# Feed-forward products of a two-layer trunk: columns walked in 14 orders, low parts of the weights at six starts

## The chip, the core and the metric

The kernel runs on one core of a Trainium2 chip. The metric is the device time of one execution in microseconds (us). The kernel before was timed twice: 1116.48 and 1116.37 us, median 1116.42 us. The core's engines are TensorE (PE: matmuls, and PEld: the loads of the stationary operand), VectorE (DVE), ScalarE (ACT), GpSimd (POOL) and SyncE (SP, which issues transfers).

## The reference

Two layers over a sequence of 512 tokens of width 1024, all in float32. Each layer has an attention part (stick-breaking heads and differential heads, one shared input and one shared output projection) and a feed-forward part. The change lies in the feed-forward part alone:

```python
h = rmsnorm(x, mlp_norm[l])
u = jnp.square(jax.nn.relu(jnp.einsum('bsd,df->bsf', h, w_ff1[l])))   # 1024 -> 4096
x = x + jnp.einsum('bsf,fd->bsd', u, w_ff2[l])                        # 4096 -> 1024
```

A final rmsnorm follows the second layer.

## The kernel before, in words

**Split operands.** Every float32 operand of a product is split into a high part, rounded to the type in which TensorE works here (`fp32r`), and a low part, the rest of it: `whi` and `wlo` for weights, `h_hi`/`h_lo` or `hxh`/`hxl` for the normed input and `Ah`/`Al` for the hidden values. A product is then three matmuls, high by high, high by low and low by high, accumulated in one PSUM tile. They are issued by the helper `three` (L298 to L304); so the three lines L302, L303 and L304 carry nearly all matmuls of the program, and the profile's groups are told apart by the tiles' names.

**Units.** The weights come in units of 128 x 1024 values. `_unit_list` (L53) writes their order out by hand, and the class `_Weights` (L95) loads, splits and hands them out in that order. `split_part` (L120) takes a pair of tiles from a pool, lets ACT write the high part (L118) and DVE the low part (L135). A low tile is 1152 columns wide, 128 more than a unit, so that the 1024 columns can begin at some column other than 0. Before, they begin at column 16 for the kinds `s` and `v` and at column 0 for all others (`NARROW`, `ASIDE`, L40, used in L128).

**The feed-forward part** works in four groups `g`, each of a quarter of the 4096 hidden values. Both products are made with seven multiplications of blocks in place of eight; the seven are the *forms* 11, x3, x2, 21, x1, x4 and 22.

- Group 0's first product is plain: units of kind `1`, 128x512 matmuls into tiles called `f`. The change doesn't touch them.
- First product of groups 1 to 3: units of kind `s`, 84 in all (two layers, three groups, two halves `j`, seven forms), in `quad_group` (L1050). Here the weights are stationary (128x128) and the normed input is moving: 256 columns, one row of a tile, without a gap. A unit makes 24 matmuls: two halves `pr` of the PSUM tile, four blocks of depth, three matmuls each. Sums go to the PSUM tiles X, V and Y.
- Second product, all groups: units of kind `f`, 112 in all (two layers, four groups, seven forms, two halves `c`), in the loop over `FORMS2` (L1235 on). Here the hidden values are stationary and the weights are moving: 512 columns. A unit makes 12 matmuls: two rows of weights, two blocks of tokens that go to two PSUM banks in turn, three matmuls each. Sums go to X, V, Y, W and, for the last unit pair, Z; the last pair's second block of tokens is cut into two halves of 256 columns (`part`).

**Order.** The program order of each engine is that of the code, with some edges added by hand (`behind`). After each unit's use `next` (L158) asks for the split of the unit that lies some units ahead; the loads of later weights hang on that split (`then`). In the attention part a planner with costs fills TensorE's queue; the feed-forward part has a fixed order.

**Matmuls in the attention part that the prediction uses as yardsticks.** L552 (`scores`) reads a moving operand of two runs of 128 columns that lie apart in SBUF, and writes 256 PSUM columns in one run. L302, L303, L683 and L684 with 128x512 into the tiles called `O0d` and `O0s` (`s3`) read two runs of 256 columns that lie 640 apart (`firsts`). L554 and L555 read one run. L441 and L442 (`values_of`) have the weights, units of kind `v`, as moving operand: L441 reads `wlo`, which begins at column 16, and L440 and L442 read `whi`, which begins at column 0.

Of the kernel before, what the change touches and what calls it, by code (L numbers as in the profile page):

```python
# [24 lines left out]
GROUPS = 4  # L25
# [11 lines left out]
MAN = ()  # L37
APART = (("s", 0, 1), ("s", 3, 0), ("s", 3, 1))
_CTX = {}
NARROW, ASIDE = "sv", 16  # L40
DLY_R, DLY_D, DLY_S, DLY_Q = 3.5, 10.2, 9.0, 6.0
TAIL, ATT, DENSE, CAP = 6.0, 53.0, 145.0, 0.1
FORMS = ("11", "x3", "x2", "21", "x1", "x4", "22")
FORMS2 = ("11", "x3", "21", "x2", "x1", "x4", "22")
# [40 lines left out]
_UNITS = _unit_list()  # L85


_INDEX = {u: i for i, u in enumerate(_UNITS)}
_RING = [i for i, u in enumerate(_UNITS) if u[0] not in "fs"]
_SLOT = {u: n for n, u in enumerate(_RING)}  # L90
# [4 lines left out]
class _Weights:  # L95
# [24 lines left out]
    def split_part(self, i, a, b):  # L120
        nc = self.nc
        if i not in self.tiles and i in self.home:
            self.tiles[i] = self.home[i]
        if i not in self.tiles:
            k = self.spot(i)
            self.owner[k] = i
            self.turn = k + 1
            at = ASIDE if _UNITS[i][0] in NARROW else 0  # L128
            hi = self.pools[k // 2].tile([P, 1024], F32R, tag="whi", name=f"whi{i}")
            lo = self.pools[k // 2].tile([P, 1152], F32R, tag="wlo", name=f"wlo{i}")[:, at : at + 1024]  # L130
            self.tiles[i] = (hi, lo)
        hi, lo = self.tiles[i]
        raw = self.first if (i, b) == (0, P) else self.raw[i]
        h = self.round(hi[:, a:b], raw[:, a:b])
        self.last = h, nc.vector.tensor_tensor(  # L135
            out=lo[:, a:b], in0=raw[:, a:b], in1=hi[:, a:b].bitcast(F32), op=ALU.subtract)
# [21 lines left out]
    def next(self, kind, alone=False):  # L158
        i = self.used
        assert _UNITS[i][0] in kind  # L160
        self.used += 1
        if i > 0 and not alone:
            self.do_split(i + 2 * len(self.pools), i)
        return self.tiles.pop(i)
# [3 lines left out]
def trunk(ctx, tc, opened, xT, w, w2, w1, gfin, lamv, cos, sin, out):  # L168
# [71 lines left out]
    def split(hi, lo, src):  # L240
        a = nc.scalar.activation(hi, src, AF.Copy)  # L241
        nc.vector.tensor_tensor(out=lo, in0=src, in1=hi.bitcast(F32), op=ALU.subtract)  # L242
        return a
# [51 lines left out]
            nc.tensor.transpose(pt[:, j * P : (j + 1) * P], col[:, j : j + 1].to_broadcast([P, P]), ident)  # L295
        nc.scalar.copy(bc, pt)

    def three(pt, a, b, first, last, goes_on=False):  # L298
        ah, al = a
        bh, bl = b  # L300
        return (
            nc.tensor.matmul(pt, ah, bh, start=first, stop=False, skip_group_check=goes_on),  # L302
            nc.tensor.matmul(pt, ah, bl, start=False, stop=False, skip_group_check=goes_on),  # L303
            nc.tensor.matmul(pt, al, bh, start=False, stop=last, skip_group_check=goes_on))  # L304
# [4 lines left out]
    def wpair(u, c, n=P):  # L309
        return u[0][:, c * n : (c + 1) * n], u[1][:, c * n : (c + 1) * n]  # L310
# [27 lines left out]
    for l in range(L):  # L338
        with ExitStack() as actx:
# [49 lines left out]
            first = W.split  # L389
# [459 lines left out]
            at = attn()  # L849
# [3 lines left out]
            for cost in dense(pts if l else None):  # L853
# [5 lines left out]
                while live and credit > 0:  # L859
                    c = next(at, None)  # L860
# [17 lines left out]
        with ExitStack() as fctx:  # L878
# [3 lines left out]
            last = l == L - 1  # L882
# [157 lines left out]
            def temp(k, name):  # L1040
                if k == 3:
                    return bank("o", name)
                while ring[0] % 3 != k:
                    bank("s", "skip")
                return bank("s", name)

            def chunk(j, k):
                return x[:, ((4, 5, 6, 7), (4, 5, 0, 1))[j][k], :]

            def quad_group(g, j, banks_):  # L1050
                nm = f"{l}{g}{j}"
                X, V, Y = (temp(k, f"{n}{nm}") for k, n in zip(banks_, "XVY"))
                sx, v3 = x[:, 2, :], x[:, 3, :]
                F = [chunk(j, k) for k in range(4)]
                both = x[:, 4:8, :].rearrange("p (a b) t -> p a b t", b=2)[:, :, 0, :]
                if j:
                    both = x.rearrange("p (a b) t -> p a b t", b=4)[:, :, 0, :]
                hi, lo = ([e[:, k, :, :].rearrange("p a t -> p (a t)") for k in range(7)] for e in sides[j])
                for form in FORMS:
                    u = W.next("s")  # L1060
                    to = {"x3": V, "x4": V, "21": Y}.get(form, X)
                    h = h_forms[form]
                    for pr in range(2):
                        for c in range(4):
                            at = 512 * pr + P * c
                            three(to[:, 256 * pr : 256 * pr + 256], (u[0][:, at : at + P], u[1][:, at : at + P]),
                                  (h[0][:, c, :], h[1][:, c, :]),
                                  form in ("11", "x3") and pr == c == 0, pr == 1 and c == 3, True)
                    if form == "11":
                        nc.scalar.copy(Y, X)  # L1070
                    elif form == "x3":
                        nc.scalar.copy(v3, V)
                    elif form == "x2":
                        nc.scalar.copy(sx, X)
                    elif form == "21":
                        nc.scalar.activation(F[1], Y, AF.Relu)
                        nc.scalar.activation(F[1], F[1], AF.Square)
                        split(hi[0], lo[0], F[1])
                    elif form == "x1":
                        nc.vector.scalar_tensor_tensor(  # L1080
                            out=F[2], in0=X, scalar=-1.0, in1=v3, op0=ALU.mult, op1=ALU.subtract)
                    elif form == "x4":
                        tt2(F[0], V, sx, ALU.add)
                        nc.scalar.activation(both, both, AF.Relu)
                        nc.scalar.activation(both, both, AF.Square)
                        split(hi[1], lo[1], F[2])
                        tt2(F[1], F[1], F[0], ALU.subtract)
                        tt2(F[0], F[2], F[0], ALU.subtract)
                        tt2(F[2], F[2], F[1], ALU.add)
                        split(sides[j][0][:, 3:5, :, :].rearrange("p k a t -> p (k a t)"),  # L1090
                              sides[j][1][:, 3:5, :, :].rearrange("p k a t -> p (k a t)"),
                              x[:, 4:6, :].rearrange("p c t -> p (c t)"))
                    else:
                        nc.scalar.activation(F[3], X, AF.Relu, scale=-1.0)
                        nc.scalar.activation(F[3], F[3], AF.Square)
                    if j and form in ("11", "x3", "x2"):
                        rest_of_forms(0, {"11": "21", "x3": "x2", "x2": "22"}[form])
# [112 lines left out]
            for g in range(GROUPS):  # L1210
# [24 lines left out]
                for form in FORMS2:  # L1235
                    total, to = SUMS[form], chains[CHAIN[form]]
                    opens = form == "11" or g == 0 and form in ("x3", "21")
                    if form == "x4" and not end:
                        to = [temp(k, f"W{l}{g}{k}") for k in (r_, s_)]
                        opens = True  # L1240
                    work = [(c, i, r, 0) for c in range(GP // 2) for i in range(2) for r in range(2)]
                    tail = end and form == "22"
                    if tail and last:
                        turned = gather(total, to)
                        to = [temp(k, f"Z{l}{k}") for k in (r_, s_)]
                        opens = True
# [9 lines left out]
                    for n, (c, i, r, part) in enumerate(work):  # L1256
                        if c not in held:
                            held[c] = W.next("f")
                        u = held[c]
                        hi, lo = (e[:, :, i, :] for e in sides[c])  # L1260
                        rs = slice(r * P, r * P + P)
                        mine = [m for m, e in enumerate(work) if e[2:] == (r, part)]
                        pt, b_ = to[r], wpair(u, i, 512)
                        if part:
                            pt = halves[part - 1][:, 0:256]
                            b_ = [e[:, 256 * part - 256 : 256 * part] for e in b_]
                        three(pt, (hi[:, SIDE[form], rs], lo[:, SIDE[form], rs]), b_,
                              opens and n == mine[0] and part < 2, n == mine[-1], not opens)
                        if tail and last and n == 3:
                            squares += [square(0, 0), seed, square(1, 0)]  # L1270
                            first += [weighed[2], turned[1], came[1], root(0), weighed[3], root(1), store(0, 0, False)]
                            squares.append(store(0, 1, True))
                            first += [*gather(total, to, (0,)), store(1, 0, False)]
                            squares += [square(2, 1), store(1, 1, True)]
                        if end and not last and form == "22" and n % 2:
                            h = back(n // 2)
                            rests.append(h[1])
                            halfway = h
# [21 lines left out]
                    elif end and last and form == "x4":  # L1300
                        first = [came[0]]
# [97 lines left out]
```

## Time and profile before

| what | value |
|---|---|
| median of the timed runs | 1116.42 us (1116.37 to 1116.48) |
| the profiled execution's own time | 1116.32 us |
| its span, first to last instruction | 1114.6 us |
| TensorE matmuls | 6345, busy 1106.9 us |
| layer 1's feed-forward part on TensorE | 236.85 to 553.88 us |
| layer 2's feed-forward part on TensorE | 788.48 us to the end |

In the profile a group of instructions is given as line, engine, operation, written tile, read tiles, shape and count, then busy time in us and mean duration of one in ns, then the engine's idle time ahead of them. TensorE's matmuls overlap: one starts before the end that the profile models for its predecessor, so the *step* from one start to the next is what a matmul costs, and the duration is the step and a fixed tail.

### The profile page before, as it was taken

Reading aid. Unit: us, or ns where it says so; the run is one execution under the profiler, and the core shown is the slowest. Engines: PE = TensorE matmul, PEld = TensorE weight load, DVE = VectorE, ACT = ScalarE, POOL = GpSimd, SP = SyncE. Lnnn points to the kernel's source line nnn. Section 1 sums busy time; section 2 is a strip of 40 time slices with the busy share of each in tenths; the row PEclk is TensorE's granted clock in tenths of the full one; section 3 lists DMA queues with packets and bytes.
Section 4 is the critical chain, followed back from the end, with each engine's and each line's share of the span. In section 5 each row is a group of like instructions: output and inputs, shape, how many; then the busy total and the mean of one; then the engine's idle time right before and its main releaser. Section 6 shows DMA issues by size and latency. Waiting matters only on the chain.

```text
span 1114.6 us, 17170 instructions
## 1 busy us (share of the span) xinstructions
PE 1106.9 (99%) x6345; PEld 968.2 (87%) x6345; DVE 908.6 (82%) x1333; ACT 689.6 (62%) x1131; POOL 151.8 (14%) x233
## 2 busy tenths in 40 slices
PE   9999999999999999999999999999999999999997
PEld 6889889888899899899878898988888998998986
DVE  7799788898668779779877897897797787797797
ACT  6447767567558458467345576775774484674765
POOL 1001343101011001001000014430010010010010
PEclk9999999999999999999999999999999999999999
DMA  7476343269687778648325654512577886697462
GB/s 241 147 189 189 114 131 107 84 220 228 176 216 179 179 202 188 190 133 214 109 76 150 188 159 129 168 60 76 210 172 186 207 183 182 185 189 206 116 132 95
DMA packets 61044, 181.25 MB, mean 163 GB/s; under 512 B 7456, under 2 KB 8736, under 8 KB 60960
## 3 DMA queue, kind: packets, MB, share of 16 engines
q1 hardware_dynamic: 50160, 141.84, 40.2%
q0 software_dynamic: 10368, 37.75, 19.6%
q8 instruction: 50, 0.82, 0.3%
q10 hardware_dynamic: 432, 0.56, 0.1%
q14 instruction: 34, 0.28, 0.1%
HBM read 150.77 MB, written 4.19 MB: 139 GB/s over the span
## 4 chain that ended last, share of the span: by engine, by line
PE 96%; DVE 2%; issue 1%; DMA 0%; ACT 0%; POOL 0%; SPq 0%; POOLq 0%; DVEq 0%; ACTq 0%
PE X L302 9%; PE X L304 9%; PE X L303 9%; PE V L302 4%; PE V L304 4%; PE V L303 4%; PE wo L302 3%; PE wo L303 3%; PE wo L304 3%; PE f L304 3%; PE f L302 3%; PE f L303 3%; PE Y L304 2%; PE Y L303 2%; PE Y L302 2%; PE W L304 1%
## 5 line engine op out<-in xcount | busy, mean ns | idle before, releaser
L118 ACT ACTIVATE whi<-q 128x1024 fp32r<-128x1024 f32 x96 | 101.7, 1059 | 106.1 <-PE X L304 38.0
L135 DVE TENSOR_TENSOR wlo<-q,whi 128x1024 fp32r<-128x1024 f32 x96 | 117.2, 1222 | 44.6 <-ACT whi L118 44.3
L118 ACT ACTIVATE whi<-raw 128x1024 fp32r<-128x1024 f32 (+1 forms) x82 | 81.0, 994 | 34.5 <-issue 17.9
L135 DVE TENSOR_TENSOR wlo<-raw,whi 128x1024 fp32r<-128x1024 f32 (+1 forms) x82 | 96.7, 1186 | 6.7 <-ACT whi L118 6.4
L302 PE MATMUL X<-whi,Ah 128*128 128x512 f32 x248 | 97.5, 393 | 0.0
L303 PE MATMUL X<-wlo,Ah 128*128 128x512 f32 x248 | 96.6, 390 | 0.0
L304 PE MATMUL X<-whi,Al 128*128 128x512 f32 x248 | 96.6, 390 | 0.0
L135 DVE TENSOR_TENSOR wlo<-waves,whi 128x1024 fp32r<-128x1024 f32 x40 | 48.9, 1222 | 15.9 <-ACT whi L118 15.8
L118 ACT ACTIVATE whi<-waves 128x1024 fp32r<-128x1024 f32 x40 | 42.3, 1056 | 29.1 <-PE X L304 20.5
L302 PEld LDWEIGHTS X<-whi,Ah 128*128 128x128 f32 x248 | 46.5, 188 | 12.0 <-DVE y L1123 1.9
L304 PEld LDWEIGHTS X<-whi,Al 128*128 128x128 f32 x248 | 46.6, 188 | 9.9
L303 PEld LDWEIGHTS X<-wlo,Ah 128*128 128x128 f32 x248 | 46.6, 188 | 8.9
L304 PE MATMUL X<-h_hi,wlo 128*128 128x256 f32 x192 | 54.1, 282 | 0.0
L304 PE MATMUL X<-hxh,wlo 128*128 128x256 f32 x192 | 54.1, 282 | 0.0
L303 PE MATMUL X<-h_lo,whi 128*128 128x256 f32 x192 | 54.0, 281 | 0.0
L302 PE MATMUL X<-hxh,whi 128*128 128x256 f32 x192 | 54.0, 281 | 0.0
L303 PE MATMUL X<-hxl,whi 128*128 128x256 f32 x192 | 54.0, 281 | 0.0
L302 PE MATMUL X<-h_hi,whi 128*128 128x256 f32 x192 | 53.9, 281 | 0.0
L302 PE MATMUL f<-h_hi,whi 128*128 128x512 f32 x128 | 50.4, 393 | 0.0
L304 PE MATMUL f<-h_hi,wlo 128*128 128x512 f32 x128 | 49.9, 390 | 0.0
L303 PE MATMUL f<-h_lo,whi 128*128 128x512 f32 x128 | 49.8, 389 | 0.0
L242 DVE TENSOR_TENSOR Al<-x,Ah 128x512 fp32r<-128x512 f32 (+1 forms) x60 | 46.5, 792 | 3.7 <-ACT Ah L241 3.5
(764 smaller groups left out, 3693.3 us busy)
## 6 DMA issues: line engine op xcount, KB each, us to landing
raw<-in_w SPq DMA_DIRECT2D x78, 512.0 KB, 3.6
q<-in_w SPq DMA_DIRECT2D x48, 512.0 KB, 4.3
q<-in_w POOLq DMA_DIRECT2D x48, 512.0 KB, 7.8
waves<-in_w SPq DMA_DIRECT2D x28, 512.0 KB, 4.5
first_a<-in_w SPq DMA_DIRECT2D x12, 512.0 KB, 5.1
first_b<-in_w SPq DMA_DIRECT2D x12, 512.0 KB, 5.3
first_c<-in_w SPq DMA_DIRECT2D x12, 512.0 KB, 4.1
first_b<-in_w POOLq DMA_DIRECT2D x12, 512.0 KB, 6.3
```

The costliest lines, as they stand in the source:

```text
L118: return self.nc.scalar.activation(o, src, AF.Copy)
L135: self.last = h, nc.vector.tensor_tensor(out=lo[:, a:b], in0=raw[:, a:b], in1=hi[:, a:b].bitcast(F32), op=ALU.subtract)
L242: nc.vector.tensor_tensor(out=lo, in0=src, in1=hi.bitcast(F32), op=ALU.subtract)
L302: nc.tensor.matmul(pt, ah, bh, start=first, stop=False, skip_group_check=goes_on),
L303: nc.tensor.matmul(pt, ah, bl, start=False, stop=False, skip_group_check=goes_on),
L304: nc.tensor.matmul(pt, al, bh, start=False, stop=last, skip_group_check=goes_on))
```

## The change

Two things change, both for the units of kinds `s` and `f` alone.

1. **Orders of walking.** `three` gets an argument `way`. With it the columns of the PSUM tile and of the moving operand (high and low) are visited in another order, the same for both, so each product still lands in its own column. A way is (a, c, back): the columns are cut into runs of c neighbouring columns, and the runs are taken in order (a = 1), or interleaved from `a` stretches; `back` turns the order of the runs ("b"), of the stretches ("a"), or of the columns inside each run ("c", the only ways in which neighbouring columns are visited downwards). The number of matmuls, of columns and of bytes is as before. `WAYS1` serves the `s` units (256 columns), `WAYS2` the `f` units (512 columns); entry 0 of each is the old order.
2. **Starts of the low parts.** The low part of an `s` unit begins at column 0, 8, 16, 24, 32 or 64 of its tile, that of an `f` unit at 0, 8, 16 or 32. Kind `v` stays at 16, all others at 0.

`_turn_of` numbers the 84 `s` units as 14 ways times 6 starts, and the `f` units as 14 ways times 4 starts (the two halves `c` share one). The halves of the last unit pair (`part`) keep the old order.

```diff
-NARROW, ASIDE = "sv", 16
+ASIDE = 16
+WAYS1 = ((1, 256, ""), (1, 32, "b"), (2, 32, ""), (4, 32, ""), (2, 16, ""),
+         (2, 64, ""), (4, 8, ""), (2, 8, ""), (4, 16, ""), (1, 32, "c"),
+         (1, 64, "c"), (2, 32, "a"), (8, 16, ""), (2, 32, "b"))
+PLACES1 = (0, 8, 16, 24, 32, 64)
+WAYS2 = ((1, 512, ""), (1, 128, "b"), (2, 32, ""), (4, 32, ""), (2, 16, ""),
+         (2, 128, ""), (8, 32, ""), (2, 8, ""), (4, 64, ""), (1, 32, "c"),
+         (1, 128, "c"), (2, 64, "a"), (16, 16, ""), (1, 64, "b"))
+PLACES2 = (0, 8, 16, 32)
...
+def _turn_of(u):
+    l, g = u[1], u[2]
+    if u[0] == "s":
+        n = ((l * 3 + g - 1) * 2 + u[3]) * 7 + FORMS.index(u[4])
+        return WAYS1[n % len(WAYS1)], PLACES1[n // len(WAYS1)]
+    n = (l * GROUPS + g) * 7 + FORMS2.index(u[3])
+    return WAYS2[n % len(WAYS2)], PLACES2[n // len(WAYS2)]
...
-            at = ASIDE if _UNITS[i][0] in NARROW else 0
+            kind = _UNITS[i][0]
+            at = _turn_of(_UNITS[i])[1] if kind in "fs" else ASIDE if kind == "v" else 0
...
-    def three(pt, a, b, first, last, goes_on=False):
+    def walked(t, way):
+        a, c, back = way
+        if c == t.shape[-1]:
+            return t
+        if a == 1:
+            t = t.rearrange("p (b c) -> p b c", c=c)
+            return t[:, ::-1, :] if back == "b" else t[:, :, ::-1] if back == "c" else t
+        t = t.rearrange("p (a b c) -> p b a c", a=a, c=c)
+        return t[:, ::-1, :, :] if back == "b" else t[:, :, ::-1, :] if back == "a" else t
+
+    def three(pt, a, b, first, last, goes_on=False, way=None):
         ah, al = a
         bh, bl = b
+        if way:
+            pt, bh, bl = (walked(e, way) for e in (pt, bh, bl))
...
                             three(to[:, 256 * pr : 256 * pr + 256], (u[0][:, at : at + P], u[1][:, at : at + P]),
                                   (h[0][:, c, :], h[1][:, c, :]),
-                                  form in ("11", "x3") and pr == c == 0, pr == 1 and c == 3, True)
+                                  form in ("11", "x3") and pr == c == 0, pr == 1 and c == 3, True,
+                                  _turn_of(("s", l, g, j, form))[0])
...
-                              opens and n == mine[0] and part < 2, n == mine[-1], not opens)
+                              opens and n == mine[0] and part < 2, n == mine[-1], not opens,
+                              None if part else _turn_of(("f", l, g, form, c))[0])
```

## The prediction

> **What bounds the kernel now.** I read the page first: the busy times, the granted clock and the chain of work that ended last.
>
> ```profile
> span 1114.6 us, 17170 instructions
> ...
> PE 1106.9 (99%) x6345; PEld 968.2 (87%) x6345; DVE 908.6 (82%) x1333; ACT 689.6 (62%) x1131; POOL 151.8 (14%) x233
> ...
> PEclk9999999999999999999999999999999999999999
> ...
> PE 96%; DVE 2%; issue 1%; DMA 0%; ACT 0%; POOL 0%; SPq 0%; POOLq 0%; DVEq 0%; ACTq 0%
> ```
>
> TensorE is busy for 1106.9 of 1114.6 us, its clock is never held down (every slice of PEclk reads 9), and 96% of the chain runs through it. Busy does not mean at its peak, so next I cut the span at the seams of the feed-forward stages and read the busy time of each stretch. The columns are the stretch, its length, and then busy time and count for each engine; the last three are granted clock, DMA share and GB/s.
>
> ```profile
> 280.85:319.11 38.26, 38.26 (x169) 31.40 (x168) 24.96 (x26) 21.95 (x27) 3.50 (x4) 1.00 0.76 193
> 319.11:358.69 39.58, 39.58 (x338) 39.57 (x336) 30.02 (x32) 29.47 (x39) 5.32 (x7) 1.00 0.75 189
> ...
> 874.43:914.01 39.58, 39.58 (x338) 39.58 (x336) 31.29 (x34) 28.69 (x37) 5.29 (x7) 1.00 0.76 189
> 914.01:952.37 38.36, 38.36 (x170) 31.42 (x169) 31.58 (x35) 19.02 (x22) 3.41 (x4) 1.00 0.76 191
> ```
>
> The stretches from 280.85 and 914.01 are second products (`f` units, 14 units of 12 matmuls = 168); those from 319.11 and 874.43 are first products (`s` units, 14 of 24 = 336; the count of PE holds one or two neighbours that reach over the seam, that of PEld doesn't). In all four TensorE is busy for the whole length: no matmul waits for anything. So a nanosecond that a walked matmul gains or loses stands in the end time one for one, and whatever the other engines do inside their spare time is worth nothing.
>
> The prices follow. A 256-column matmul of an `s` unit costs 39.58 / 336 = 117.8 ns from start to start. A 512-column matmul of an `f` unit costs 38.26 / 168 = 227.7 ns. The difference, 109.9 ns for 256 columns, is 0.429 ns for a column; what is left of the short one, 117.8 - 109.9 = 7.9 ns, is fixed for each matmul. These are the two things on which a walk can act: time per column and time per instruction.
>
> **The change part by part.** It adds and removes no instruction, no transfer and no wait, and it moves none past another in any queue. It changes the address sequence of some matmuls and the address of some tiles.
>
> *How many.* Entry 0 of each list is the old order. Of 84 `s` units 6 keep it, so 78 x 24 = 1872 matmuls are walked. Of 112 `f` units 8 keep it; the other 104 make 1248, less 12 whose tokens are cut into unwalked halves: 1236. Together 3108 of 6345.
>
> *How many jumps.* A jump is a place where the next run doesn't follow the last one. A way with runs of c columns has 256/c - 1 or 512/c - 1 of them. Over the 14 ways that sums to 155 for `s` and 215 for `f`. Each way has 6 `s` units (144 matmuls) and 8 `f` units (96): 155 x 144 + 215 x 96 - 84 (the unwalked halves) = 42,876 jumps.
>
> *What a jump of the moving operand costs.* The trace has matmuls that already read two runs: L552 (two of 128, by the code) and the 128x512 ones into O0s and O0d (two of 256). Beside them stand one-run matmuls of the same sizes: L554 and L555 from the same stage, and the groups that the change touches.
>
> ```profile
> L552 PE MATMUL S0s<-st0s3k,st0s3q 128*128 128x256 f32 x2 | 0.6, 278 | 0.0
> L554 PE MATMUL S0s<-st0s3k,st0s3q 128*128 128x256 f32 x2 | 0.6, 281 | 0.0
> L683 PE MATMUL O0s<-turned,vs 128*128 128x512 f32 x5 | 2.0, 392 | 0.0
> L302 PE MATMUL O0d<-turned,vdh 128*128 128x512 f32 x4 | 1.6, 391 | 0.0
> L303 PE MATMUL O0d<-turned,vdh 128*128 128x512 f32 x4 | 1.6, 392 | 0.0
> L554 PE MATMUL S0s<-st0s3k,st0s3q 128*128 128x512 f32 x2 | 0.8, 393 | 0.0
> L555 PE MATMUL S0s<-st0s3k,st0s3q 128*128 128x512 f32 x2 | 0.8, 389 | 0.0
> ...
> L302 PE MATMUL X<-whi,Ah 128*128 128x512 f32 x248 | 97.5, 393 | 0.0
> L303 PE MATMUL X<-wlo,Ah 128*128 128x512 f32 x248 | 96.6, 390 | 0.0
> L302 PE MATMUL X<-hxh,whi 128*128 128x256 f32 x192 | 54.0, 281 | 0.0
> ```
>
> With one jump: 278 ns at 256 columns, 391 to 392 at 512. With none: 281, and 389 to 393. So a jump costs between -3 and +3 ns by single rows, and nothing that stands out of their scatter. I take 0: the mean is below it at 256 columns and within it at 512. A gain from jumps I exclude, since every column still has to pass. For the upper end I take 1 ns, about what the 512-column rows leave (391.7 on the mean of the three with a jump, 391 of L554 and L555): 42,876 x 1 ns = +42.9 us.
>
> *What the walked PSUM side costs.* No matmul of the trace writes its PSUM columns in more than one run, and none goes downwards, so no row prices this. The floor is 0, from the moving side just read: the array takes a column every 0.429 ns, and the write needs only to keep that pace. The ceiling by the nearest rows is a second pass of the columns, 109.9 ns for a 256-column matmul and 219.8 for a 512-column one; I keep it for the rivals. I take 0, because each run holds at least 8 neighbouring columns and the two-run rows show address generation keeping pace on the reading side. That is the weakest step of this prediction.
>
> *Two orders on one bank.* Consecutive units add into the same tile in different orders, so a column could be asked for again sooner than before. It is not: the three matmuls of one product share an order, an `s` unit ends in the second half of its tile while the next begins in the first, and an `f` unit alternates between two banks. Cost 0.
>
> *The starts.* An `s` unit's low part is stationary in L304. These are the weight loads of that line and of L302, and the moving low part in the `v` units:
>
> ```profile
> L304 PEld LDWEIGHTS X<-hxh,wlo 128*128 128x128 f32 x192 | 36.9, 192 | 0.0
> L302 PEld LDWEIGHTS X<-hxh,whi 128*128 128x128 f32 x192 | 36.0, 188 | 0.0
> L304 PEld LDWEIGHTS f<-h_hi,wlo 128*128 128x128 f32 x128 | 24.0, 188 | 5.1
> ...
> L441 PE MATMUL p0u<-wlo,h_hi 128*128 128x256 f32 x64 | 17.9, 280 | 0.0
> L442 PE MATMUL p0u<-whi,h_lo 128*128 128x256 f32 x64 | 17.9, 280 | 0.0
> ```
>
> Low parts that begin at column 16 load in 192 ns, those at 0 (`f<-h_hi,wlo`) in 188. If the start is the reason, and if the whole of it lies on the path, 70 of 84 units leave column 16: 70 x 8 x 4 ns = 2.2 us gained. If every other start loads like 16, nothing. I take 0 and keep -2.2 us as the lower bound, because one row cannot tell the start from the place in the triple. As a moving operand a low part at column 16 costs what a high part at 0 does (280 and 280 ns), so the `f` units' starts are free. For the writer:
>
> ```profile
> L135 DVE TENSOR_TENSOR wlo<-q,whi 128x1024 fp32r<-128x1024 f32 x96 | 117.2, 1222 | 44.6 <-ACT whi L118 44.3
> L135 DVE TENSOR_TENSOR wlo<-first_a,whi 128x1024 fp32r<-128x1024 f32 x24 | 29.4, 1225 | 20.6 <-ACT whi L118 20.6
> ```
>
> DVE writes at column 16 (`first_a`) in 1225 ns and at 0 (`q`) in 1222: 3 ns on some 200 writes, 0.6 us, covered by VectorE's spare 9.6 us in each stretch of 39.58 (30.02 busy). Without that cover it would be those 0.6 us.
>
> **Sum.** 0 (jumps) + 0 (PSUM) + 0 (order) + 0 (starts), on the profiled execution's own 1116.32 us: span 1114.6 and 1.7 around it. The median of the timed runs lies 0.1 above, so the forecast is 1116.4 us. Its own range is 1114 (2.2 for the starts) to 1121 (a quarter of a column, 0.107 ns, for each jump: 4.6 us). About 2%, 22.3 us here, is what a measurement of this kernel can tell from no change.
>
> **Rivals.**
>
> *Every jump costs a little.* One mechanism, the address generator restarting at each run, on reading or writing. At one column (0.429 ns) it is 18.4 us, 1134.8; at 1 ns 42.9 us, 1159.3. It decides from 22.3 us / 42,876 = 0.52 ns on. For it: the two-run 512 rows are a shade above some one-run rows. Against: L552 at 278 ns is below.
>
> *Downward columns pass at half pace.* Two of the 14 ways ("c") visit neighbouring columns downwards: 12 `s` units (288 matmuls) and 16 `f` units (192). If the PSUM write or the read takes neighbours in pairs and pairs only upwards, each pays a second pass: 288 x 109.9 ns + 192 x 219.8 ns = 73.9 us, 1190.2. It decides from 30% of such a pass on. For it: the trace has no downward matmul. Against: nothing but that no engine here shows a price for order as such. The Trainium skill, Advanced Engine Details and Errata, section PSUM Cachelines, wants "every two consecutive elements" to be contiguous; twelve ways satisfy that, and it doesn't say whether a downward pair does.
>
> *Every broken write passes at half pace.* All 3108 walked matmuls pay the second pass: 1872 x 109.9 ns + 1236 x 219.8 ns = 477.4 us, 1593.8. The same section also says that any non-contiguous access pattern slows matmuls significantly; by that sentence alone this rival holds, and no run here shows a broken PSUM write. Against: runs of 8 and more give the write the same neighbours as before, except once per run.
>
> *Faster.* If walking hid the fixed 7.9 ns of each walked matmul (say, by meeting a memory line that is free sooner), it would give 3108 x 7.9 = 24.6 us, 1091.8. Against: the two-run rows keep it; L552's 3 ns would be a third of it at best.
>
> *The change does nothing at all* gives the forecast's time too; it is part of the first case.
>
> **How the numbers follow.** Forecast 0.70; a price for each jump 0.12, a third of it below 0.52 ns and so within 2%; downward half pace 0.11; half pace for all 0.04; faster 0.03. Faster by over 2%: 0.03. Within: 0.70 + 0.04 = 0.74. Slower: 0.08 + 0.11 + 0.04 = 0.23. The range goes from 1113.5, the lower bound of the starts with half a microsecond for the repeat, to 1160, the price of 1 ns for each jump: 0.70 + 0.12 = 0.82 lie in it.
>
> **What would show it.** In the changed profile the same stages should have the same lengths (39.58 and 38.3 us), TensorE without idle time, and each group of L302, L303 and L304 the durations quoted. A price for each jump shows as units whose matmuls last longer the shorter their runs are, most in those with runs of 8. Downward half pace shows as two units in 14 at twice the step, and none elsewhere. A start that matters shows in the loads of L304 alone, 188 or 192 ns by unit. The forecast is wrong if the stretches grow, and which of the rivals is right is read from which units grow.

## The result, and the profile after

The changed kernel takes 1128.84 us (1128.74 to 1128.94), against 1116.42 before: a ratio of 1.0112, 95% interval 1.0095 to 1.0128. That is 12.4 us slower. It lies inside the range given, but the forecast was no change, and the kernel moved by more than its runs scatter. That it lies in the range is luck: the upper end came from a price for each jump, which the experiments below rule out as the cause.

The profile page of the changed kernel, the lines that answer to those of before:

```profile
span 1127.0 us, 17170 instructions
...
PE 1119.5 (99%) x6345; PEld 972.3 (86%) x6345; DVE 909.0 (81%) x1333; ACT 690.5 (61%) x1131; POOL 152.0 (13%) x233
...
PEclk9999999999999999999999999999999999999999
...
PE 99%; issue 0%; DVE 0%; POOL 0%; ACT 0%; POOLq 0%; DVEq 0%; ACTq 0%
```

The count of instructions is the same, the clock is the same, and TensorE's busy time has grown by 12.6 us, the span by 12.4. DVE and ACT have hardly grown (0.4 and 0.9 us, off the path). The stages, with the same columns as in the prediction:

```profile
280.75:319.94 39.19, 39.19 (x169) 31.50 (x168) 24.96 (x26) 22.00 (x27) 3.50 (x4) 1.00 0.74 191
319.94:360.14 40.20, 40.20 (x338) 40.19 (x336) 30.02 (x32) 29.57 (x39) 5.38 (x7) 1.00 0.75 187
...
881.48:921.56 40.08, 40.08 (x337) 40.08 (x336) 31.17 (x34) 28.85 (x37) 5.33 (x7) 1.00 0.75 186
921.56:961.11 39.55, 39.55 (x171) 31.47 (x170) 31.74 (x35) 19.06 (x22) 3.37 (x4) 1.00 0.72 184
```

TensorE is still busy for their whole length; each matmul is a little dearer. The 14 `f` units of the first line went from 38.26 to 39.19 us, the 14 `s` units of the second from 39.58 to 40.20. Summed from start to start over the whole trace, `s` matmuls grew from 237.4 to 240.7 us and `f` matmuls from 306.8 to 316.2: 3.2 and 9.3 us, together all of it but for rounding (differences taken before rounding; the `f` sums count the halves of the last unit pair too).

Cutting the changed trace at single groups of 24 `f` matmuls (two units of one form) shows something that the prediction had ruled out. The columns here are the stretch, its length, TensorE's busy time and count, and the clock, DMA share and GB/s:

```profile
280.75:286.19 5.44, 5.44 (x25) 1.00 0.60 99
286.19:291.63 5.44, 5.44 (x25) 1.00 0.61 162
...
439.46:445.02 5.56, 5.56 (x26) 1.00 1.06 205
...
841.89:847.45 5.56, 5.56 (x26) 1.00 0.55 80
1001.25:1006.85 5.60, 5.60 (x27) 1.00 1.04 202
```

The first, third, fourth and fifth are all in the old order (way 0); their low parts start at 0, 8, 16 and 32. At start 0 the group takes 5.44 us, as before, and at the others 5.56 to 5.60. Against the same groups of the kernel before (5.44 to 5.47 us) that is 4.0 to 5.4 ns a matmul from the start alone. The second is walked in reversed runs of 128, at start 0, and costs nothing.

### The profile page after: what moved, and what is told of

It reads as the page before. It is cut to its first block, busy times and chain, and to the rows that moved or that the text cites. A ratio compares the mean times of both kernels' runs of the same rounds, so it can differ in the third digit from the quotient of the medians.

```text
span 1127.0 us, 17170 instructions
## 1 busy us (share of the span) xinstructions
PE 1119.5 (99%) x6345; PEld 972.3 (86%) x6345; DVE 909.0 (81%) x1333; ACT 690.5 (61%) x1131; POOL 152.0 (13%) x233
## 4 chain that ended last, share of the span: by engine, by line
PE 99%; issue 0%; DVE 0%; POOL 0%; ACT 0%; POOLq 0%; DVEq 0%; ACTq 0%
PE X L332 9%; PE X L334 9%; PE X L333 9%; PE V L334 4%; PE V L332 4%; PE V L333 4%; PE wo L332 3%; PE wo L333 3%; PE wo L334 3%; PE f L334 3%; PE f L332 3%; PE f L333 3%; PE Y L332 2%; PE Y L333 2%; PE Y L334 2%; PE W L333 1%
## 5 line engine op out<-in xcount | busy, mean ns | idle before, releaser
L334 PE MATMUL X<-whi,Al 128*128 128x512 f32 x248 | 98.6, 398 | 0.0
L334 PEld LDWEIGHTS X<-whi,Al 128*128 128x128 f32 x248 | 46.7, 188 | 11.6
L334 PE MATMUL X<-h_hi,wlo 128*128 128x256 f32 x192 | 54.4, 284 | 0.0
L334 PE MATMUL X<-hxh,wlo 128*128 128x256 f32 x192 | 54.3, 283 | 0.0
L334 PE MATMUL f<-h_hi,wlo 128*128 128x512 f32 x128 | 49.9, 390 | 0.0
```

## The experiments

**Theory 1, phase.** TensorE's step depends on how the address of the operand that streams in stands to the address of the operand that is being loaded for the next matmul, within some period. Starts and walks both disturb a relation that the kernel before had tuned. **Theory 2** is the rival of the prediction: a price for each jump of a walk, and starts for nothing.

### Starts and walks apart

*walks_only*, against the changed kernel:

```diff
-            at = _turn_of(_UNITS[i])[1] if kind in "fs" else ASIDE if kind == "v" else 0
+            at = ASIDE if kind in "sv" else 0
```

> The walks as in the change, the starts as before (s at 16, f at 0). Theory 1, phase: TensorE slows where the address phase of the moving operand against the other operands leaves the one tuned before, whether by a start or by a walk; the changed profile's units that kept the old start (f units of layer 1, groups 0 and 1: on the mean 5.6 ns a matmul over the 14 ways; s units with start 16: 1.5 ns) give 1332 x 5.6 + 2016 x 1.5 = 7.5 + 3.0 = 10.5 us, so about 1126.9 us, with the ways (1, 128, b) and (1, 64, b) of the f units free although they have 3 and 7 jumps. Theory 2, a price for each jump and starts for nothing: the whole 12.4 us, 1128.8 us. If walks were free and starts the whole cause: 1116.4 us.

Measured: 1126.92 us, ratio 1.0096 (1.0081 to 1.0111), 10.4 us over the kernel before on the same chip.

*starts_only*, against the changed kernel:

```diff
-        if way:
+        if way and False:
```

> The starts as in the change, all walks in the old order. Theory 1, phase: the units that had way 0 in the changed kernel price this, f 0, 4.0, 5.0 and 5.4 ns a matmul at starts 0, 8, 16 and 32, s 1.6, 0.5, 0.0, 0.9, 1.3 and 1.6 ns at 0, 8, 16, 24, 32 and 64: 1332 x 3.6 + 2016 x 1.0 = 6.8 us, about 1123.2 us. Theory 2, a price for each jump: 1116.4 us. My prediction's own reading of the starts (free but for 2.2 us of gain): 1114 to 1116.4 us.

Measured: 1122.95 us, ratio 1.0060 (1.0045 to 1.0075), 6.4 us over. Both came out where theory 1 put them. Its sums were made of prices read in the changed trace, so these two runs show that walks and starts each have a price of their own; the phase itself is tested further down. The starts' part is 4.1 us in the `f` matmuls and 2.5 us in the `s` matmuls (steps summed over the trace). The two prices add up to 16.8 us, and together in the change they cost 12.4. By theory 1 this is because a pair of addresses that is already off its tuned phase can't leave it a second time; that reason is argued, not shown.

The stages of *starts_only*, whose units are all in the old order, read the starts off one by one:

```profile
280.69:318.96 38.27, 38.27 (x169) 31.40 (x168) 24.95 (x26) 21.97 (x27) 3.50 (x4) 1.00 0.77 194
318.96:359.27 40.31, 40.31 (x337) 40.31 (x336) 30.03 (x32) 29.61 (x39) 5.38 (x7) 1.00 0.75 189
...
437.43:476.52 39.09, 39.09 (x171) 31.43 (x169) 31.73 (x35) 19.00 (x22) 3.42 (x4) 1.00 0.73 186
476.52:516.10 39.58, 39.58 (x338) 39.58 (x337) 31.20 (x34) 28.70 (x37) 3.60 (x5) 1.00 0.62 173
```

`f` at 0: 38.27 us, as before; `s` at 0: 40.31, 0.7 more than before; `f` at 8: 39.09, 0.7 more; `s` at 16, its old start: 39.58, as before.

The weight loads of the second stage (`s` at 0) and of the fourth (`s` at 16) differ too. Shown is a load of `whi` in the second, then the same in the fourth:

```profile
L333 PEld LDWEIGHTS X<-h_lo,whi 128*128 128x128 f32 x32 | 6.1, 192 | 0.0
```

```profile
L333 PEld LDWEIGHTS X<-h_lo,whi 128*128 128x128 f32 x32 | 6.0, 188 | 0.0
```

The high part begins at column 0 in both, and still its load takes 4 ns more when the low part moves from 16 to 0. The low part's own load (L334) takes 192 ns in both. So a load's time is not a matter of its own start alone.

In *walks_only* every `f` unit starts at 0, so the groups of 24 matmuls price the ways. These are the seven of layer 1's group 0: old order; 128 reversed (3 jumps); then interleaved runs of 32, 32, 16, 128 and 32 (15, 15, 31, 3 and 15 jumps):

```profile
280.63:286.07 5.44, 5.44 (x25) 1.00 0.52 93
286.07:291.51 5.44, 5.44 (x25) 1.00 0.63 163
291.51:297.20 5.69, 5.69 (x26) 1.00 0.68 112
297.20:302.80 5.60, 5.60 (x26) 1.00 0.98 344
302.80:308.66 5.86, 5.86 (x26) 1.00 0.60 187
308.66:314.15 5.49, 5.49 (x25) 1.00 0.95 198
314.15:319.83 5.68, 5.68 (x26) 1.00 0.89 237
...
376.83:382.43 5.60, 5.60 (x26) 1.00 0.83 272
...
393.81:399.25 5.44, 5.44 (x26) 1.00 0.91 236
```

(Of the fifth line 0.10 us is a wait, one step of 339 ns where the others take 240; the kernel before has it in the same place, 337 ns.) The last two lines are from group 1: (1, 128, c), runs of 128 downwards, 3 jumps, 5.60; and (1, 64, b), runs of 64 in reversed order, 7 jumps, 5.44. So 7 jumps can cost nothing, and 3 can cost 6.6 ns a matmul; the three ways with 15 jumps take 5.69, 5.60 and 5.68. What the free ones share is upward runs of whole multiples of 64 columns. Both downward ways settle at 233.3 ns, with 3 jumps and with 15, and no run separates the direction from the phase there. The line at 5.49, upward interleaved runs of 128, is one of the free ones too. Cut in halves it reads:

```profile
308.66:311.44 2.78, 2.78 (x14) 1.00 0.95 140
311.44:314.15 2.71, 2.71 (x13) 1.00 0.94 258
```

Its first twelve matmuls still carry the state that the unit before it left behind; from the eleventh on the steps repeat 226, 227, 227 ns, the old rhythm (2.71 us for twelve). All five of the `f` units' ways with upward runs of multiples of 64 end in that rhythm, and none of the other walks does.

In the `s` units the rule is looser. There (2, 64) stays at the old 117.8 ns, but so do upward runs of 32 in (2, 32) and downward runs of 64 in (1, 64, c). The reversed runs of 32, (1, 32, b), settle at 116.7 ns, which is faster than the old order, and (2, 8) at 123.3.

### The period of 64 columns

*start_curve*, against the changed kernel: no walks, and

```diff
-        return WAYS1[n % len(WAYS1)], PLACES1[n // len(WAYS1)]
+        return WAYS1[0], n
...
-    return WAYS2[n % len(WAYS2)], PLACES2[n // len(WAYS2)]
+    return WAYS2[0], 2 * n
```

> All walks in the old order; each of the 56 form groups of f units has a start of its own, 0, 2, 4 to 110 columns, and each of the 84 s units one from 0 to 83. Theory 1, phase with a period of 64 columns (256 bytes): f units at 0 and at 64 step at 226.7 ns, and the cost at k equals that at k + 64; s units at 16 and at 80 step at 117.8 ns, and those at 64 to 83 step as those at 0 to 19. Rival, any start other than the one before costs: f at 64 and s at 80 as slow as their neighbours, by about 5 and 1 ns. The whole lands between 1120 and 1128 us by either.

Measured: 1123.33 us. The `s` units (24 matmuls each) that start at 0, 16, 36, 64 and 80:

```profile
319.72:322.58 2.86, 2.86 (x25) 1.00 0.19 79
404.41:407.24 2.83, 2.83 (x26) 1.00 1.03 313
500.42:503.21 2.79, 2.79 (x27) 1.00 0.00 0
980.12:983.00 2.88, 2.88 (x27) 1.00 0.54 82
1064.73:1067.56 2.83, 2.83 (x27) 1.00 0.10 19
```

0 and 64 are alike, 16 and 80 are alike. In the last twelve matmuls of each of the units from 64 to 83 the mean step stands within 0.1 ns of that of the unit 64 columns below, in 20 of 20 (120.0 and 120.0, 117.8 and 117.8, 118.3 and 118.3, and so on). The `f` groups at 0 and 64 end at 226.7 and 227.5 ns; the others lie between 228.8 and 236.7, but for one of 245 in layer 1's last stage, where waits fall in that the kernel before has as well (the last group, with its halves, is left aside). Of the 23 pairs of `f` groups that lie 64 columns apart 17 agree to 0.2 ns at their ends; the other six differ by 0.6 to 3.3 ns, so for `f` the curve bears the period out only in the main.

*start_plus64*, against the changed kernel: no walks, and

```diff
-            at = _turn_of(_UNITS[i])[1] if kind in "fs" else ASIDE if kind == "v" else 0
+            at = ASIDE + 64 if kind == "s" else 64 if kind == "f" else ASIDE if kind == "v" else 0
```

> All walks in the old order; f units start at 64 in place of 0, s units at 80 in place of 16. Theory 1, phase with a period of 64 columns: nothing changes, 1116.4 us. Rival, any start other than the one before costs: f 4.8 ns x 1332 = 6.4 us and s 1 ns x 2016 = 2 us, about 1124.8 us.

Measured: 1116.26 us, ratio 0.9999 (0.9989 to 1.0008). Sixty-four columns, 256 bytes, are a whole period. Thirty-two are not, as the runs with a shift of 32 show further down.

### Which side of a walk pays

*walk_moving_only* and *walk_psum_only*, both with the old starts, against the changed kernel:

```diff
-            pt, bh, bl = (walked(e, way) for e in (pt, bh, bl))
+            bh, bl = walked(bh, way), walked(bl, way)      # walk_moving_only
+            pt = walked(pt, way)                           # walk_psum_only
```

> Starts as before; the moving operand is walked as in the change, the PSUM tile in the old order, so that the sums land in other columns than they should. Theory 1, phase of TensorE's reads from SBUF: the cost of the walks stays whole, 10.4 us, 1126.9 us, with the same steps in each unit. Rival, the price is paid where PSUM is written: 1116.4 us.

> Starts as before; the PSUM tile is walked as in the change, the moving operand is read in the old order, so that the sums land in other columns than they should. Theory 1, phase of TensorE's reads from SBUF: no cost, 1116.4 us. Rival, broken or downward writes to PSUM cost: up to 1126.9 us, most in the units with the shortest runs.

Measured: 1126.80 us, ratio 1.0095 (1.0075 to 1.0115), and 1116.23 us, ratio 1.0000 (0.9990 to 1.0010). The first two feed-forward stages of each, moving side first:

```profile
281.22:320.41 39.19, 39.19 (x169) 31.49 (x168) 24.96 (x26) 21.99 (x27) 3.50 (x4) 1.00 0.76 194
320.41:360.48 40.07, 40.07 (x337) 40.06 (x336) 30.03 (x32) 29.58 (x39) 5.39 (x7) 1.00 0.76 186
```

```profile
281.04:319.31 38.27, 38.27 (x170) 31.39 (x168) 24.96 (x26) 21.97 (x27) 3.50 (x4) 1.00 0.76 194
319.31:358.88 39.57, 39.57 (x337) 39.57 (x336) 30.02 (x32) 29.46 (x39) 5.35 (x7) 1.00 0.73 187
```

Reading carries the whole price; writing PSUM in broken runs, runs of 8 and downward columns among them, costs nothing. The Trainium skill's sentence that any non-contiguous access pattern significantly slows matmuls (Advanced Engine Details and Errata, PSUM Cachelines) doesn't hold here; its other sentence there, that every two consecutive elements should be contiguous, stands with the run, if a downward pair counts.

### Against which operand

*weights32*, against the kernel before, moves both parts of the `f` units' weights:

```diff
-            at = ASIDE if _UNITS[i][0] in NARROW else 0
-            hi = self.pools[k // 2].tile([P, 1024], F32R, tag="whi", name=f"whi{i}")
-            lo = self.pools[k // 2].tile([P, 1152], F32R, tag="wlo", name=f"wlo{i}")[:, at : at + 1024]
+            at = 32 if _UNITS[i][0] == "f" else ASIDE if _UNITS[i][0] in NARROW else 0
+            by = 32 if _UNITS[i][0] == "f" else 0
+            hi = self.pools[k // 2].tile([P, 1088], F32R, tag="whi", name=f"whi{i}")[:, by : by + 1024]
+            lo = self.pools[k // 2].tile([P, 1088], F32R, tag="wlo", name=f"wlo{i}")[:, at : at + 1024]
```

*sides32*, against the kernel before, moves the hidden values instead:

```diff
+            fp.tile([P, 32], F32, tag="pad0", name=f"pad0{l}")
             sides = [[fp.tile([P, 7, 2, 256], F32R, tag=f"A{n}{j}", name=f"A{n}{j}_{l}") for n in "hl"] for j in range(2)]
+            fp.tile([P, 32], F32, tag="pad1", name=f"pad1{l}")
```

*all32* has both edits.

> The kernel before, with the high and the low part of every f unit both starting at column 32 (tiles of 1088 columns each). Theory 1a, what counts is the phase of the moving operand against the stationary one that is being loaded: all f matmuls leave the tuned phase, 2 to 7 ns x 1332, 1119 to 1126 us. Theory 1b, what counts is the phase between the two moving parts that follow one another: they keep it, 1116.4 us.

> The kernel before, with the tiles of the hidden values (stationary in the f units) moved by 32 columns, 128 bytes, by a pad tile ahead of them and one behind; the weights stay at 0. Theory 1a, phase of the moving operand against the stationary one: with a period of 64 columns, +32 of the one is -32 of the other, so it costs what moving both parts of the weights by 32 costs, with the same steps. Theory 1b, phase between the two moving parts: 1116.4 us.

> The kernel before, with the hidden values' tiles and both parts of the f units' weights all moved by 32 columns. Theory 1a, only the phase of the moving operand against the stationary one counts, and here it is the old one: 1116.4 us, f matmuls back at 226.7 ns. Rival, the place of an operand itself counts (some columns of the memory are slower, or the pads and tile sizes did it): as slow as with one of the two moved, 1122.8 to 1123.6 us.

Measured: *weights32* 1122.76 us, ratio 1.0060 (1.0040 to 1.0080); *sides32* 1123.56 us, 1.0066 (1.0046 to 1.0086); *all32* 1115.95 us, 0.9999 (0.9989 to 1.0009). The first `f` stage of each, in this order:

```profile
281.21:320.45 39.24, 39.24 (x170) 31.44 (x168) 24.96 (x26) 22.00 (x27) 3.50 (x4) 1.00 0.76 191
```

```profile
280.43:319.60 39.17, 39.17 (x169) 31.50 (x168) 24.96 (x26) 21.99 (x27) 3.49 (x4) 1.00 0.75 190
```

```profile
280.29:318.57 38.28, 38.28 (x169) 31.40 (x168) 24.95 (x26) 21.95 (x27) 3.50 (x4) 1.00 0.77 193
```

Moving either operand costs 6.6 or 7.3 us, moving both costs nothing. That takes away three other causes at once: the place of an operand by itself, the relation of the high part to the low part (it is kept in *weights32*), and the pads and tile sizes (they are in *all32*). TensorE reads the hidden values through its weight loads alone in this stage, and beside it only eight operations of ACT and DVE touch their tiles, against 168 matmuls that nearly all step longer. So it is the stream of a matmul and the load for the next one that meet. The expectation of the same steps in *weights32* and *sides32* held in kind only: the same values recur, in other sequences, and the sums differ by 0.6 us.

The Trainium skill (TensorE: Matmul & The Clock Gate, Step-by-step: what each phase is for) says that loading the next weights doesn't take read bandwidth from the running matmul. No run here measures the bandwidth. But 128 bytes between the two are worth 6.6 and 7.3 us, and the measurement decides: the two are not independent here.

### Can the phase be tuned further?

*s36*, against the kernel before, moves the low part of the `s` units to the column that looked best in the curve:

```diff
-            at = ASIDE if _UNITS[i][0] in NARROW else 0
+            at = 36 if _UNITS[i][0] == "s" else ASIDE if _UNITS[i][0] == "v" else 0
```

> The kernel before, with the low part of every s unit at column 36 in place of 16. The curve of starts had the unit with 36 at 115.6 ns a matmul against 117.8. Theory 1: 2016 x 2.2 ns = 4.4 us gained, 1112.0 us. If the 115.6 ns was a chance of its neighbours in the curve: 1116.4 us.

Measured: 1116.38 us, ratio 1.0001 (0.9991 to 1.0010). A miss. With every unit at 36 the steps settle to another rhythm (116 to 120 ns, mean 117.8) than that unit had in the curve (112 to 118, mean 115.6). So the phase doesn't decide alone.

*both_curve* moves high and low part together, by 0 to 55 columns in the `f` groups and by 0 to 63 and 0 to 19 in the `s` units, with the tiles of *weights32* (the diff is cut to the two starts; `_turn_of` gives each unit its column there):

```diff
+            at = _turn_of(_UNITS[i]) if _UNITS[i][0] in "fs" else ASIDE if _UNITS[i][0] == "v" else 0
+            by = at if _UNITS[i][0] in "fs" else 0
```

> All walks in the old order; the high and the low part of an f unit both start at one column, 0, 1, 2 to 55 by form group, and those of an s unit at 0 to 63, then 0 to 19 again. Theory 1a: f groups at 0 step at 226.7 ns and at 32 as in the run with both parts at 32 (about 231 to 233 ns); the cost depends on the start finely, not in steps of 8. For s the low part against the high part is 0 at every start, so s units differ only by the phase against the normed input: if that counts they spread by some ns, as f units do; if only low against high counts they all step at 120 ns, as the curve's start 0. The whole lies between 1116 and 1126 us.

Measured: 1124.64 us. `f` groups at 0 stepped at 226.7 ns and at 32 at 232.5 ns, as expected, and no start beat 0. The `s` units spread from 113.3 to 122.7 ns, so it is not low against high alone that counts. These are the `s` units at 13, 16, 19, 13, 16 and 19, the last three 64 units later in the program:

```profile
357.24:359.98 2.74, 2.74 (x26) 1.00 1.05 197
404.82:407.65 2.83, 2.83 (x27) 1.00 1.00 308
413.33:416.05 2.72, 2.72 (x26) 1.00 1.07 229
1057.55:1060.30 2.75, 2.75 (x27) 1.00 0.02 6
1065.99:1068.72 2.73, 2.73 (x26) 1.00 0.14 17
1074.40:1077.12 2.72, 2.72 (x26) 1.00 1.23 234
```

At 16 the same phase gives 2.83 us in one place and 2.73 in the other: more than one rhythm is stable there. What picks is not shown: the units ahead of both start at 15 and take 119.6 and 119.7 ns. At 13 and 19 both visits are short.

*s_both13* and *s_both19* give one of these to all `s` units, against the kernel before (13 here; the tiles are again those of *weights32*, cut here):

```diff
+            by = 13 if _UNITS[i][0] == "s" else 0
+            at = by or ASIDE * (_UNITS[i][0] == "v")
```

> The kernel before, with both parts of every s unit at column 13 (tiles of 1088 columns each). In the curve with both parts moved, the units at 13 and at 77 settled to 113.3 ns a matmul after some six matmuls of 115 to 120, from different entries. If the phase alone decides: 2016 x (117.8 - 113.5) = 8.7 us gained, about 1107.5 us. If the state at entry decides, as with the start 36: 1116.2 us.

> The same with column 19, where the units at 19 and at 83 of the curve stepped at 113.3 ns from their first matmul on. If the phase alone decides: about 8.7 us gained, 1107.5 us. If the state at entry decides: 1116.2 us.

Measured: *s_both13* 1120.96 us, ratio 1.0042 (1.0029 to 1.0054), slower; *s_both19* 1107.69 us, ratio 0.9927 (0.9913 to 0.9940), 8.3 us faster than the kernel before and 21 faster than the changed one. The second stage of each:

```profile
319.34:359.67 40.33, 40.33 (x338) 40.33 (x337) 30.04 (x32) 29.64 (x39) 5.38 (x7) 1.00 0.75 189
```

```profile
318.91:357.00 38.09, 38.09 (x337) 38.09 (x336) 29.83 (x32) 29.18 (x39) 5.25 (x6) 1.00 0.76 192
```

38.09 / 336 = 113.4 ns a matmul, against 117.8 before. At 13 every unit falls into a rhythm of 120 ns, though the two units in the curve, entered from other starts, had fallen into 113.3 and 113.6. At 19 the short one is reached after the first three matmuls of a stage and kept. So the phase doesn't decide alone at 13, and 19 was short in every entry that was tried.

## Why the prediction was wrong

- **What bounds the kernel** was right: TensorE had no slack in these stages, every nanosecond of its step came out in the end time (12.6 us of busy time, 12.4 us of span), and nothing off TensorE mattered. One reading in it was too strong: from a busy time of the whole length I took that no matmul waits. The profile's matmuls overlap by some 166 ns (393 against a step of 227), so a shorter wait doesn't show as idle time. In the first `f` stage of the kernel before one matmul steps 337 ns, its load having waited 0.30 us for ACT. It is there before and after, so it doesn't touch the sum.
- **What a jump of the moving operand costs: "I take 0"** is the step that failed, for 10.4 us of walks. The yardsticks could not show the price. L552 reads two runs of 128 columns, 1024 apart, and L683 two of 256, 640 apart: whole multiples of 64 columns, in runs and in jumps. In the `f` units those are the walks that cost nothing in the experiments as well. Of the ways in the change, only a few have that property, and I used the rows as if they stood for all. The 7.6 us in the `f` matmuls and 3.0 us in the `s` matmuls of *walks_only* were paid on the reading side. "A gain from jumps I exclude" was too strong as well: (1, 32, b) made `s` matmuls 1.1 ns shorter.
- **The starts, taken at 0,** are the other, for 6.4 us alone. "So the `f` units' starts are free" failed for 4.1 us. The row for it was L441 against L442, one low part at column 16 beside a high part at 0 in one stage of the attention part. It is one phase of 64 against one kind of stationary operand, and it says nothing of the others; an `f` matmul off its tuned start costs 4.0 to 5.4 ns. For the `s` units I allowed a gain of up to 2.2 us for leaving column 16, since L304's loads took 192 ns there against 188 at column 0. It came out as a loss of 2.5 us: at start 0 the loads of all three lines take 192 ns and the matmul steps 120.0 ns against 117.8. The 4 ns were a sign of the phase, not a price of column 16.
- **PSUM, called the weakest step**, was right at 0: *walk_psum_only* is at 1.0000.
- **Two orders on one bank** was right at 0, by the same run.
- **The rivals.** A price for each jump came nearest in time: 12.4 us is 0.29 ns for each of the 42,876 jumps. But it is not the mechanism: 7 jumps were free, 3 cost 6.6 ns a matmul in a downward way, and starts without any jump cost 6.4 us. Downward half pace is out: (1, 128, c) costs 3%, not 100%. Half pace for all is out. "Faster" came near the kind of thing that moves, some ns of each matmul: up by as much as 16.6 ns in the `f` units, way (2, 8), and at start 19 down by 4.4 in the `s` units. Whether that is fixed for each matmul, like the 7.9 ns, or lies on the columns, no run separates.
- **What a measurement can tell** was put at 2%, and the rivals were weighed by it. The runs tell changes of about 0.2% (all intervals above are that narrow), so prices far below 0.52 ns a jump had to be weighed too.

## What to carry to other kernels

Where matmuls run back to back, treat the address of the streamed operand against that of the operand being loaded as a tuning knob, and scan its 64 offsets of one float32 column (256 bytes). No offset was best for both products: 0 was the best that was tried in the `f` units, while in the `s` units 0 was a slow one (120.0 ns) and 19 the best (113.4). Starts alone were worth from +7.3 us (*sides32*) to -8.3 us (*s_both19*) in 1116 here. A scan with one offset per unit ranks offsets only roughly, since one offset can have more than one rhythm, so run the winner everywhere before believing it. A row of the trace prices a new access pattern only if it differs from the old in the property that counts; several rows that agree may all share that property.

## What the runs showed of the hardware

- TensorE's step for the same matmul varies with the relation of its two reads, which has a period of 256 bytes: from 113.3 to 123.3 ns at 256 columns, where whole stages ran at 113.4, 117.8, 118.3 or 120.0, and from 226.7 to 243 at 512. For the `f` units the two reads are shown by moving each and both; for the `s` units the starts show the period, and that their moving operand is the other side is taken over from `f`.
- The load goes along with it: the same high part's load took 188 ns with the low part at column 16 and 192 with it at 0.
- The sequence of steps repeats: an `s` matmul stream walked on its moving side alone gave the same step sums in every unit as the full walk, to 0.1 ns a matmul.
- A disturbed `f` stream needed up to fourteen matmuls to find its rhythm again, where the phase allowed it; the kernel before needed five at the start of most `f` stages.
- A broken or downward PSUM write was free in runs of 8 columns and more.
- Open: what in the memory has the period of 256 bytes, what picks between two stable rhythms at one phase, and whether a downward walk of the moving operand has a price of its own. The runs show that two rhythms exist and not why.
